# A hybrid encoder trunk on one core: products b^T a of the WKV chunks made in the preparation and kept in DRAM, and both prompt jobs' inverses, first merges and loads placed among the last v products

## The chip, the cores and the metric

The kernel runs on one core of one Trainium2 chip. A core has TensorE (PE: matmuls; PEld: its weight loads), VectorE (DVE), ScalarE (ACT), GpSimd (POOL) and SyncE (SP), which here only issues DMA transfers; ACT and POOL issue some too. Each engine works through its own queue in order. The metric is the device time of one execution in microseconds (us), as the median of several runs. The kernel before takes 4056.93 us (three runs, 4045.68 to 4063.49).

## The reference

Two batches, a prompt of 256 tokens and a sample of 1024 tokens, pass through two layers with the same weights: RWKV-7 time mixing and an MLP, then neighbourhood attention and an MLP, all in float32. The change touches the time mixing alone. It ends in a scan over the tokens, run forwards and backwards for each of 16 heads of 64 channels:

```python
def step(S, inp):
    r_t, w_t, k_t, v_t, a_t, b_t = inp
    sa = jnp.einsum('bhvk,bhk->bhv', S, a_t)
    S = S * w_t[:, :, None, :] + sa[..., None] * b_t[:, :, None, :] + v_t[..., None] * k_t[:, :, None, :]
    return S, jnp.einsum('bhvk,bhk->bhv', S, r_t)
...
for d in range(2):
    w_lora = jnp.tanh(xw @ w1[d]) @ w2[d]
    decay = jnp.exp(-jnp.exp(-jax.nn.softplus(-(w0[d] + w_lora).astype(f32)) - 0.5))
    iclr = _heads(jax.nn.sigmoid((a0[d] + (xa @ a1[d]) @ a2[d]).astype(f32)))
    k_d = kf * (1.0 + (iclr - 1.0) * k_a_h)
    y = y + _wkv_scan(rf, _heads(decay), k_d, vf, -kk, kk * iclr, reverse=(d == 1))
```

## The kernel before

The projections come first; then a **preparation** makes, for 8 pairs of heads m and 2 directions d, four tensors of 128 channels by tokens (b, k, a and r, each scaled by cumulative decays) and stores them in the DRAM tensor `x_d`. It works in 48 units h (pair h // 6, token segment of 256, 512 or 512 tokens, direction h % 2). Between the units stand the r products (`rps`, three matmuls for each float32 product, L108 to L110) and, from unit 42.5 on, the 40 blocks of v products (`vps`, 24 matmuls each, L530 to L532), which go on when the units are done. All this is placed by a list `self.cq` of (time in units, function): it is sorted, and what it calls is the written order of PE, DVE, ACT and POOL (`manual_schedule`). SP is not in that set; its order comes from the scheduler.

The **scan** cuts tokens into chunks of 64. Within a chunk the recurrence is solved as a triangular system: its matrix is built from the 64 x 64 products b^T a of the chunk, and its inverse Q is needed before the chunk's step. Ten jobs of 16 chunks follow each other: jobs 0 and 1 hold the prompt (4 pairs with 4 chunks each), jobs 2 to 9 the sample of one pair each. Each job has 16 steps, and each step handles one chunk forwards and one backwards for both heads of the pair (or of a prompt pair). What a job needs is placed in a second list, `todo`, by time in steps (job j at 16 j, earlier parts at negative times):

- `load` (L844): a and b of 4 chunks from `x_d` into `eab`, 256 KB, four buffers; eight loads per job.
- `early` (L850): b^T a, eight matmuls of 64 x 64 into the PSUM tile `aps` per load (each float32 matmul shows as two rows); `keep` (L854) copies them to `za` on ACT; `store` (L857) writes them to the DRAM tensor `dd` of the job.
- `mload` (L877): the 32 x 32 diagonal blocks of a job's systems are gathered from `dd`, one system on each partition, into `mt` and `mraw`; `mtr` (L882) transposes `mraw` into `mt` on POOL in four pieces.
- `rank1` (L895 to L901): the inverse of all 32 x 32 blocks in 31 steps on DVE, 60 instructions.
- `qst` (L909 to L912): the inverses go to the DRAM tensor `qd`, transposed by POOL as well; `qld` (L927, L928) loads them into `Q` and `qx` in 12 transfers of 64 KB in pieces of 32 numbers.
- `merge1`, `merge2` (L940 to L954): the 64 x 64 inverse from its 32 x 32 blocks, with `za` and `qx`, eight groups per job on PE and ACT (`yps`, `qps`).
- `kload`, `decay` (L966, L971): k, b, a, r of 4 chunks into `x` (512 KB), and the decay matrix into its fifth part by POOL; `uvload` and `vload` (L979, L1017): v from DRAM.
- `kprod`, `kcopy`, `kmask` (L995, L1005, L1000): products of each pair of chunks into the one PSUM tile `kps`, copied by ACT (`ll`) and masked by DVE (`zz`).

The step itself is a chain on PE and ACT: `bx` and `by` matmuls (L1033), the copies `up` (L1074, one per step), `uv` (L1086) and `S` (L1099). The output is normed and stored by `scan_post`, and gate, output projection, MLP and layer 1 follow.

When `begin` runs (unit 52, after v block 15), the preparation's memory is released, the scan's first tiles are opened in `er` (the pool that exists while v products still run; the pool `rp` opens after them), and what job 0 needs up to its inverse is moved from `todo` into `cq`, spread over the last v blocks.

Of the kernel before, what the change touches and what calls it, by code (L numbers as in the profile page):

```python
# [5 lines left out]
F32 = mybir.dt.float32  # L6
# [7 lines left out]
P = 128  # L14
# [4 lines left out]
L = 64  # L19
# [42 lines left out]
class Trunk:  # L62
# [50 lines left out]
    def l0_proj(self):  # L113
# [267 lines left out]
        for h in range(N):  # L381
# [99 lines left out]
        def begin():  # L481
            bctx.close()
            self.scan_begin()

            hi, c = -6.0, ((-46.0, tb), (-22.0, tb + 6.0), (-6.0, tb + 17.0))
            for x in self.todo:
                if x[3] < 3 and x[0] <= hi:
                    (x0, t0), (x1, t1) = c[:2] if x[0] < -22.0 else c[1:]
                    t = t0 + (t1 - t0) * (x[0] - x0) / (x1 - x0)
                    self.cq.append((max(t, t1 - 3.0 + 0.01 * x[0]) if x[3] == 2 else t, x[1], x[2]))  # L490
            self.todo = [x for x in self.todo if x[3] == 3 or x[0] > hi]
            self.cq.sort(key=lambda x: x[:2])
# [169 lines left out]
    def prep_products(self, U, h, i):  # L662
# [52 lines left out]

    def prep_bonus(self, U, h, step):
# [20 lines left out]
    def scan_begin(self):  # L737
# [8 lines left out]
        self.r_v, self.r_q, self.r_x = ([[er.tile(shape, F32, name=name + "0")], 0] for name, shape in  # L746
                                        (("vv", [P, 16, 64]), ("qq", [P, 16, 2, 64]), ("qx", [P, 16, 2, 32])))
        self.r_e = [[er.tile([P, 2, 4, 64], F32, name=f"eab{i}") for i in range(4)], 0]
        self.r_za = [[er.tile([P, 4, 64], F32, name=f"za{i}") for i in range(9)], 0]
# [5 lines left out]
        self.todo = []  # L755
# [7 lines left out]
    def scan_until(self, t, level=3):  # L763
        todo = [x for x in self.todo if x[0] <= t and x[3] <= level]
        self.todo = [x for x in self.todo if x[0] > t or x[3] > level]
        for x in todo:
            x[2]()

    def scan(self):
# [3 lines left out]
        def grow(r, name, shape, n=1):  # L773
# [1245 lines left out]
```

## Time and profile before

| what | us |
|---|---|
| median of three runs | 4056.93 |
| profiled execution, its own time | 4067.45 |
| profiled execution, span from first to last instruction | 4065.7 |
| preparation up to the first v block | about 317 to 559 |
| v blocks | 559.4 to 715.1 |
| first step of the scan (first copy `up`) | 764.3 |
| last step of the scan | 1360.0 |

Over the whole span PE is busy for 92%, DVE 62%, ACT 37%, POOL 35%. A busy time is the union of an engine's instructions; matmuls overlap, so a busy PE is not PE at its peak. The rows that follow below are of four kinds: stretches with the busy time of each engine, the granted TensorE clock (1.00 is 2.4 GHz, 0.50 is 1.2 GHz) and the share of the DMA engines; single instructions in order of time; the chain of waits, which says what released what; and DMA transfers by line, with the time from issue to landing.

### The profile page before, as it was taken

What the parts mean: (1) busy time and instruction counts of PE and PEld (TensorE: products, weight loads), DVE (VectorE), ACT (ScalarE), POOL (GpSimd) and SP (SyncE); (2) the same over time, 40 slices, a digit from 0 to 9 for tenths busy, and PEclk for the clock granted to TensorE, in tenths of its full rate; (3) what the DMA queues carried; (4) which work ended last, traced back from release to release, by engine and by line L of the source; (5) the groups of instructions that cost most, each with busy time, mean ns of one, the idle gap of its engine ahead of it and who ended that gap; (6) DMA issues with size and microseconds to landing.
All of it is one profiled execution on the core that took longest, in us unless ns stands there. A gap on an engine that the chain in (4) does not pass through costs nothing.

```text
span 4065.7 us, 82648 instructions
## 1 busy us (share of the span) xinstructions
PE 3743.1 (92%) x33028; PEld 3107.9 (76%) x33028; DVE 2508.8 (62%) x4771; ACT 1512.1 (37%) x3587; POOL 1412.1 (35%) x1402
## 2 busy tenths in 40 slices
PE   7888979688788799999999989999989999999999
PEld 4665659566667688888888879777768788888888
DVE  7898973477686447555555561466674755555555
ACT  6776652344444441121111132456564211111111
POOL 4450000245455534222222250455553422222222
PEclk8997889799999899999999999999989999999999
DMA  3326655888876431111111115343343111111101
GB/s 109 88 81 220 210 188 159 196 212 198 197 197 155 139 120 32 37 42 42 32 42 42 37 62 175 84 90 82 71 117 130 48 41 42 37 37 42 42 32 63
DMA packets 405745, 403.44 MB, mean 99 GB/s; under 512 B 163152, under 2 KB 328240, under 8 KB 404080
## 3 DMA queue, kind: packets, MB, share of 16 engines
q1 hardware_dynamic: 349488, 318.31, 28.6%
q10 hardware_dynamic: 46704, 61.35, 4.4%
q0 software_dynamic: 9168, 18.49, 1.7%
q8 instruction: 259, 4.24, 0.5%
q14 instruction: 126, 1.03, 0.1%
HBM read 288.03 MB, written 121.24 MB: 101 GB/s over the span
## 4 chain that ended last, share of the span: by engine, by line
PE 69%; DVE 14%; ACT 6%; issue 4%; DMA 4%; POOL 3%; SPq 0%; ACTq 0%; DVEq 0%; POOLq 0%
PE ps L108 18%; PE ps L109 17%; PE ps L110 17%; PE kps L995 3%; PE bx L1033 2%; PE by L1033 2%; PE vps L530 1%; PE vps L531 1%; PE vps L532 1%; PE op L1933 1%; DVE mu L199 1%; DVE q L901 1%; DVE tmp L899 1%; PE pt L1875 1%; ACT ll L1005 1%
## 5 line engine op out<-in xcount | busy, mean ns | idle before, releaser
L1480 DVE TENSOR_TENSOR x<-ps,x 128x256 f32<-128x256 f32 x1488 | 813.1, 595 | 609.9 <-PE ps L110 609.5
L103 POOL TENSOR_TENSOR wlo<-raw,whi 128x1024 fp32r<-128x1024 f32 (+1 forms) x178 | 390.7, 2195 | 851.2 <-ACT whi L102 824.4
L108 PE MATMUL ps<-ahs,whi 128*128 128x512 f32 x1536 | 612.8, 399 | 0.0
L109 PE MATMUL ps<-als,whi 128*128 128x512 f32 x1536 | 599.3, 390 | 0.0
L110 PE MATMUL ps<-ahs,wlo 128*128 128x512 f32 x1536 | 598.9, 390 | 0.0
L108 PE MATMUL ps<-hh,whi 128*128 128x512 f32 (+1 forms) x1536 | 545.2, 355 | 12.2 <-DVE x L1480 12.1
L109 PE MATMUL ps<-hl,whi 128*128 128x512 f32 (+1 forms) x1536 | 544.0, 354 | 0.0
L110 PE MATMUL ps<-hh,wlo 128*128 128x512 f32 (+1 forms) x1536 | 543.9, 354 | 0.0
L102 ACT CAST whi<-raw 128x1024 fp32r<-128x1024 f32 (+1 forms) x206 | 201.3, 977 | 692.4 <-PE ps L109 634.4
L1459 POOL TENSOR_TENSOR rl<-rl 128x512 f32<-128x512 f32 (+1 forms) x192 | 174.5, 909 | 489.9 <-PE ps L110 450.7
L108 PEld LDWEIGHTS ps<-ahs,whi 128*128 128x128 f32 x1536 | 288.7, 188 | 62.3 <-issue 6.9
L110 PEld LDWEIGHTS ps<-ahs,wlo 128*128 128x128 f32 x1536 | 288.5, 188 | 61.8
L108 PEld LDWEIGHTS ps<-hh,whi 128*128 128x128 f32 x1536 | 290.4, 189 | 55.9 <-DVE x L1480 15.6
L109 PEld LDWEIGHTS ps<-als,whi 128*128 128x128 f32 x1536 | 288.8, 188 | 53.2 <-issue 1.0
L110 PEld LDWEIGHTS ps<-hh,wlo 128*128 128x128 f32 x1536 | 290.3, 189 | 40.6
L109 PEld LDWEIGHTS ps<-hl,whi 128*128 128x128 f32 x1536 | 290.3, 189 | 40.3
L1458 ACT ACTIVATE rl<-ps 128x512 f32<-128x512 f32 (+1 forms) x192 | 100.8, 525 | 532.8 <-PE ps L110 532.8
L995 PE MATMUL kps<-x 64*64 64x192 f32 (+1 forms) x2560 | 204.9, 330 | 27.9 <-DVE zz L1000 16.2
L1461 ACT CAST hh<-rl 128x512 fp32r<-128x512 f32 (+1 forms) x192 | 105.5, 550 | 321.7 <-POOL rl L1459 321.7
L108 PE MATMUL ps<-ahp,whi 128*128 128x256 f32 x768 | 222.4, 290 | 0.8 <-DVE ot L1363 0.8
L110 PE MATMUL ps<-ahp,wlo 128*128 128x256 f32 x768 | 215.6, 281 | 1.5 <-POOL wlo L103 1.5
L109 PE MATMUL ps<-alp,whi 128*128 128x256 f32 x768 | 215.3, 280 | 0.0
(334 smaller groups left out, 8384.5 us busy)
## 6 DMA issues: line engine op xcount, KB each, us to landing
x<-x_d SPq DMA_DIRECT2D x88, 512.0 KB, 6.8
raw<-in_w_down_dram SPq DMA_DIRECT2D x64, 512.0 KB, 3.6
raw<-in_w_up_dram SPq DMA_DIRECT2D x64, 512.0 KB, 3.4
eab<-x_d SPq DMA_DIRECT2D x80, 256.0 KB, 5.1
x_d<-ar ACTq DMA_DIRECT2D x32, 512.0 KB, 3.0
x_d<-bk ACTq DMA_DIRECT2D x32, 512.0 KB, 3.9
bs<-tab SPq DMA_DIRECT2D x128, 96.0 KB, 4.9
v_d<-vt ACTq DMA_DIRECT2D x80, 128.0 KB, 3.9
```

Source lines behind the costliest of these rows:

```text
L102: nc.scalar.copy(hi[:, cs], raw)
L103: lo_eng.tensor_tensor(out=lo[:, cs], in0=raw, in1=hi[:, cs].bitcast(F32), op=ALU.subtract)
L108: mm(ps, sh, mh, start=first, stop=False)
L109: mm(ps, sh, ml, start=False, stop=False)
L110: mm(ps, sl, mh, start=False, stop=last)
L199: nc.vector.scalar_tensor_tensor(out=v, in0=sm, scalar=hm[:, i[j] * 8 + k:i[j] * 8 + k + 1], in1=v, op0=ALU.mult, op1=ALU.add)
L995: mm(J["kp"][out, e, 192 * c + 192 - w:192 * c + 192], x[es, b, 2 * pr + c], x[es, 5 - w // 64:5, 2 * pr + c], start=True, stop=True)
L1033: mm = lambda out, a, b, start, stop: nc.tensor.matmul(out, a, b, start=start, stop=stop, skip_group_check=True)
L1458: nc.scalar.activation(r[:, :n], ps[:, :n], AF.Relu)
L1459: nc.gpsimd.tensor_tensor(out=r[:, :n], in0=r[:, :n], in1=r[:, :n], op=ALU.mult)
L1461: nc.scalar.copy(hh[:, :n], r[:, :n])
L1480: nc.vector.tensor_tensor(out=xv, in0=ps[:, :n], in1=xv, op=ALU.add)
```

## The change

- **Products in the preparation.** A new DRAM tensor `za_d` holds b^T a for all pairs, directions and tokens. `prep_system` makes them in each unit: matmuls into a PSUM tile of the ring that the preparation's other matmuls use (tag `l2`, four buffers), one or two ACT copies of 256 columns, one or two DMA stores of 128 KB issued by POOL. `load`, `early`, `keep`, `store`, the tiles `eab` and the tensors `dd` are gone.
- **Reading them.** `zload` brings `za` of 4 chunks from `za_d` (128 KB, eight per job, six buffers). `mload` gathers the diagonal blocks from `za_d` in pieces of 32 numbers: eight transfers for a sample job, 32 for a prompt job, where it was four. `mt` and `mraw` are half as wide.
- **The start of the scan.** For jobs 0 and 1 `mload`, `mtr`, `rank1` and `qst` are put on the list `ahead`, which `begin` adds to `cq` at fixed times in units; so are job 0's `qclear`, `qld`, `vload`, and the merges and loads of its first two groups. The step of the list for the inverses is 4.5 units.
- **Buffers.** `er` has two tiles of `x`, one of `uv`, one of `yt` per direction, which join the rings; the last job uses none of them. The second `kd` buffer of direction 1 goes. The first merges have a PSUM pool of their own (`pmB`).

```diff
@@ in the preparation's list
             at(h + 1.191, self.prep_store, U, h, nc.scalar)
+            for i, t in enumerate((1.3, 1.75, 1.76)):
+                at(h + t, self.prep_system, U, h, i)
@@ begin
             bctx.close()
+            self.pm = vctx.enter_context(tc.tile_pool(name="pmB", bufs=2, space=PSUM))
             self.scan_begin()
-            hi, c = -6.0, ((-46.0, tb), (-22.0, tb + 6.0), (-6.0, tb + 17.0))
...
+            self.cq += [(tb + t, 1000 + i, f) for t, i, f in self.ahead]
             self.cq.sort(key=lambda x: x[:2])
@@ prep_open, prep_products
+        self.za_d = self.dram("za_d", [8, 2, P, T])
...
-            u["kd"] = pk.tile([P, 512], F32, name="kd", tag=f"kd{d}", bufs=2)
+            u["kd"] = pk.tile([P, 512], F32, name="kd", tag=f"kd{d}", bufs=2 - d)
@@ new
+    def prep_system(self, U, h, step):
+
+        nc, u = self.nc, U[h]
+        m, d, c0, c1, w = self.prep_unit(h)
+        if step == 0:
+            u["ps"] = self.ppl.tile([P, 512], F32, name="sps", tag="l2")
+            for c in range(w // L):
+                t = slice(c * L, c * L + L)
+                for es, eo in HALVES:
+                    nc.tensor.matmul(u["ps"][eo, t], u["bk"][es, 0, t], u["ar"][es, 0, t], start=True, stop=True)
+            return
+        for c in range(0, w, 256):
+            if step == 1:
+                u["za", c] = self.pk.tile([P, 256], F32, name="pza", tag="pza", bufs=2)
+                nc.scalar.copy(u["za", c], u["ps"][:, c:c + 256])
+            else:
+                nc.gpsimd.dma_start(self.za_d[m, d, :, c0 + c:c0 + c + 256], u["za", c])
@@ scan_begin, scan
-        self.r_e = [[er.tile([P, 2, 4, 64], F32, name=f"eab{i}") for i in range(4)], 0]
-        self.r_za = [[er.tile([P, 4, 64], F32, name=f"za{i}") for i in range(9)], 0]
+        self.r_za, self.r_x4, self.r_uv = ring("za", [P, 4, 64], 2), ring("x4", [P, 5, 4, 64], 2), ring("uv", [P, 8, 2, 64], 1)
+        self.r_yt = [ring(f"yt{d}", [P, 4, 64], 1) for d in range(2)]
...
-        grow(self.r_za, "za", [P, 4, 64], 12)
+        grow(self.r_za, "za", [P, 4, 64], 4)
@@ scan_job
+        pre = lambda t, f: self.ahead.append((t, len(self.ahead), f))
...
-            def early(c, x, d=d, g=g):
-                es, eo = HALVES[x]
-                if c == x == 0:
-                    J["pa"] = w4(self.pa.tile([P, 512], F32, name="aps", tag="aps"))
-                mm(J["pa"][eo, c], J["e", d, g][es, 0, c], J["e", d, g][es, 1, c], start=True, stop=True)
...
-                    nc.sync.dma_start((mt, raw)[d][o:o + 32, 32 - 32 * b:2080 - 32 * b], J["dd"][d][:, :, 32 * b:32 * b + 32].rearrange("c e s t -> (c e) (s t)"))
+                    for e in range(2):
+                        o = 64 * d + 32 * b + 16 * e
+                        for m, c0, k, n in parts:
+                            src = self.za_d[m, d, 64 * e + 32 * b:64 * e + 32 * b + 32].rearrange("s (c t) -> c s t", t=L)
+                            nc.sync.dma_start((mt, raw)[d][o + k:o + k + n], src[c0:c0 + n, :, 32 * b:32 * b + 32])
...
+        if j < 2:
+            T1, T2, T3, step, put = *((0.2, 3.0, 7.6), (8.0, 10.8, 15.4))[j], 4.5, pre
+        else:
+            T1, T2, T3, step, put = -25.2, -21.73, -9.7, 12.0, at
+        put(T1, mload)
...
+            def zload(d=d, g=g, m=m, c0=c0):
+                J["za", d, g] = self.nxt(self.r_za, left)
+                nc.sync.dma_start(J["za", d, g], self.za_d[m, d, :, tok(c0)].rearrange("p (c t) -> p c t", c=4))
...
+            t, put = 2 * n - 5, at
+            if j == 0 and n < 2:
+                t, put = 12.5 + n, pre
...
+            put(8.5 + 0.1 * n if put is pre else 2 * n - 9.5, zload)
...
+            put(10.1 + 0.1 * n if put is pre else 4 * (n // 2) - 8.5 + n % 2, kload)
+            put(10.3 + 0.1 * n if put is pre else 2 * n - 6.4, decay)
+            put(8.7 + 0.1 * n if put is pre else 4 * (n // 2) - 4.3 + 0.1 * (n % 2), uvload)
```

Three places in the written order follow. The first is PE's queue in the preparation, where two units' input products (`l<-tw`, `l<-ta`), the key norms (`kb`) and the r products (`rps`) alternate. Before:

```order
L110 MATMUL rps<-mh_233,wl 128x512
L633 MATMUL l_4619<-tw,wa 128x512
L633 MATMUL l_4622<-tw,wa 128x512
L633 MATMUL l_4626<-ta,wa 128x512
L633 MATMUL l_4630<-ta,wa 128x512
L707 MATMUL kb<-kr,heads 128x512
L108 MATMUL rps<-mh_189,wh 128x256
```

The same place now:

```order
L110 MATMUL rps<-mh_233,wl 128x512
L631 MATMUL l_5061<-tw,wa 128x512
L631 MATMUL l_5064<-tw,wa 128x512
L631 MATMUL l_5068<-ta,wa 128x512
L631 MATMUL l_5072<-ta,wa 128x512
L723 MATMUL sps<-ar,bk 64x64 x16
L705 MATMUL kb<-kr,heads 128x512
L723 MATMUL sps<-ar,bk 64x64 x8
L108 MATMUL rps<-mh_189,wh 128x256
```

Two units' b^T a (`sps`, 8 matmuls for 256 tokens and 16 for 512) now stand around `kb` and ahead of the next r products; they read `ar` and `bk`, which DVE writes.

The second place is SP's queue from the middle of the v blocks to the first loads of `x`: `wraw` are v weights, `qd` the stored inverses. Before:

```order
L877 DMA mt<-dd 32x2048
L877 DMA mraw<-dd 32x2048 x2
L410 DMA wraw<-in_w_v_dram 128x512
L844 DMA eab_6424<-x_d 128x2x256
L410 DMA wraw<-in_w_v_dram 128x512
L909 DMA qd<-q 128x1024
L912 DMA qd<-qt 128x1024
L928 DMA qq_6419<-qd 32x16x32 x2
L927 DMA qx_6420<-qd 32x16x32 x3
L928 DMA qq_6419<-qd 32x16x32
L857 DMA dd<-za_6433 128x4x64
```

Now:

```order
L901 DMA qd<-q 128x1024
L904 DMA qd<-qt 128x1024
L866 DMA mraw<-za_d 4x32x32 x8
L866 DMA mt<-za_d 4x32x32 x16
L936 DMA za_7353<-za_d 128x256
L936 DMA za_7354<-za_d 128x256
L984 DMA uv_7357<-v_d 64x4x128 x2
L1022 DMA vv_7350<-v_d 64x4x64 x8
L922 DMA qx_7352<-qd 32x16x32
L923 DMA qq_7351<-qd 32x16x32
...
L923 DMA qq_7351<-qd 32x16x32 x5
L971 DMA x_7355<-x_d 128x4x256
```

The loads of job 0's inverses (`qx`, `qq`) followed the stores of `qd` at once; now 24 of job 1's 32 gathers and 12 loads of `za`, `uv` and `vv` stand between them, and the first load of `x` stands behind all of these. The 32 gathers of job 0 are further up, where the loads of `eab` and `vv` were, ahead of the loads `wraw` that were issued at 636.56 us.

The third place is POOL's queue around the two inverses. Before:

```order
L882 COPY mt<-mraw 64x8x32 x4
L910 COPY qt<-q 128x8x32 x4
L870 MEMSET q 128x1024
L871 MEMSET q 128x32
...
L971 TENSOR_TENSOR x_7407<-cst,dall 64x256 x2
L882 COPY mt<-mraw 64x8x32 x4
L971 TENSOR_TENSOR x_7408<-cst,dall 64x256 x2
L971 TENSOR_TENSOR x_7409<-cst,dall 64x256 x2
```

Now:

```order
L870 COPY mt<-mraw 64x8x32 x4
L902 COPY qt<-q 128x8x32 x4
L856 MEMSET q 128x1024
L857 MEMSET q 128x32
L870 COPY mt<-mraw 64x8x32 x3
L976 TENSOR_TENSOR x_7355<-cst,dall 64x256 x2
L870 COPY mt<-mraw 64x8x32
L976 TENSOR_TENSOR x_7356<-cst,dall 64x256 x2
L902 COPY qt<-q 128x8x32 x4
```

The last quarter of job 1's transposing (`mt<-mraw`) now stands behind the decay matrix of `x_7355`, the first group's tile, which waits for that tile's load. On DVE all 60 instructions of job 1's inverse now stand ahead of the first mask `zz`; before, 13 of them stood ahead of it and the rest between the masks.

## Rows read from the trace of the kernel before

**Rows 1.** stretches: us, busy of PE, PEld, DVE, ACT, POOL; clock, DMA share, GB/s

```profile
360.00:540.00 180.00, 164.75 (x1049) 113.36 (x1048) 176.88 (x319) 125.55 (x268) 0.00 (x0) 0.88 0.60 206
540.00:610.00 70.00, 45.69 (x272) 36.86 (x271) 48.05 (x85) 36.20 (x75) 0.00 (x0) 0.78 0.61 190
610.00:715.00 105.00, 102.71 (x960) 100.53 (x960) 35.81 (x85) 21.80 (x54) 11.50 (x16) 0.98 0.55 157
715.00:764.00 49.00, 21.72 (x394) 19.66 (x392) 15.81 (x32) 8.71 (x24) 13.07 (x29) 0.55 0.83 201
822.00:1194.00 372.00, 306.78 (x8909) 254.62 (x8904) 282.35 (x624) 174.01 (x666) 194.36 (x284) 0.95 0.83 202
1194.00:1310.00 116.00, 99.69 (x2780) 83.14 (x2780) 86.23 (x188) 54.87 (x211) 62.12 (x88) 0.97 0.68 158
```

**Rows 2.** copies `up` that begin jobs 0, 1, 7, 9: start, us, instruction

```profile
764.28 0.27 ACT L1074 COPY up<-bx 128x128 f32<-128x128 f32 x1
821.96 0.27 ACT L1074 COPY up<-bx 128x128 f32<-128x128 f32 x1
1193.80 0.27 ACT L1074 COPY up<-bx 128x128 f32<-128x128 f32 x1
1310.28 0.27 ACT L1074 COPY up<-bx 128x128 f32<-128x128 f32 x1
```

**Rows 3.** chain of waits by line, jobs 1 to 6, then 7 and 8

```profile
by line: PE kps L995 18.8%; PE bx L1033 13.3%; PE by L1033 12.2%; issue 9.7%; DVE q L901 5.1%; DVE tmp L899 4.8%; ACT ll L1005 4.5%; DVE zz L1000 3.7%; ACT up L1074 3.0%; DMA qq<-qd 2.8%; DVE mu L1164 2.2%; PE zps L1200 1.8%; PE aps L850 1.
by line: PE kps L995 20.6%; PE bx L1033 14.5%; PE by L1033 13.8%; issue 9.1%; DVE q L901 6.2%; DVE tmp L899 5.7%; ACT ll L1005 5.3%; ACT up L1074 4.7%; DVE zz L1000 3.3%; PE zps L1200 2.6%; ACT y L1107 1.8%; ACT y L1104 1.5%; DVE mu L1164 1
```

**Rows 4.** PE in order of time, two series of b^T a

```profile
645.82 0.68 PE L850 MATMUL aps<-eab 64*64 64x64 f32 x16
722.72 3.40 PE L850 MATMUL aps<-eab 64*64 64x64 f32 x48 [5.18 <-DMA eab<-x_d]
```

**Rows 5.** stretch, instructions on `aps` alone: PE, PEld, ACT

```profile
822.00:1194.00 372.00, 35.97 (x771) 30.53 (x768) 17.49 (x48) 0.95 0.83 202
```

**Rows 6.** DVE in order of time: weights, both inverses, first mask

```profile
649.25 1.41 DVE L420 TENSOR_TENSOR wl<-wraw,wh 128x512 fp32r<-128x512 f32 x2 [9.84 <-ACT wh L415]
680.80 0.29 DVE L895 SCALAR_TENSOR_TENSOR q<-mt,q 128x31 f32<-128x31 f32 x1 [7.24 <-POOL mt L882]
705.13 0.25 DVE L895 SCALAR_TENSOR_TENSOR q<-q,mt 128x31 f32<-128x31 f32 x1
746.32 0.72 DVE L895 SCALAR_TENSOR_TENSOR q<-mt,q 128x31 f32<-128x31 f32 x1 [40.94 <-POOL mt L882]
754.32 0.68 DVE L1000 TENSOR_TENSOR zz<-kps,cst 128x512 f32<-128x512 f32 x1
```

**Rows 7.** SP's issues in order of time

```profile
626.46 9.10 SPq L1017 DMA_DIRECT2D vv<-v_d  x8
636.56 3.23 SPq L410 DMA_DIRECT2D wraw<-in_w_v_dram  x2
707.72 0.32 SPq L912 DMA_DIRECT2D qd<-qt  x1
```

**Rows 8.** POOL in order of time

```profile
678.66 2.11 POOL L882 COPY mt<-mraw 64x256 f32<-64x256 f32 x4 [53.48 <-DMA mraw<-dd]
719.29 1.29 POOL L971 TENSOR_TENSOR x<-cst,dall 64x256 f32<-64x256 f32 x2
```

**Rows 9.** DMA issues, jobs 1 to 6: KB each, median us to landing

```profile
x<-x_d SPq DMA_DIRECT2D x48, 512.0 KB, 7.4
eab<-x_d SPq DMA_DIRECT2D x48, 256.0 KB, 5.7
qq<-qd SPq DMA_DIRECT2D x48, 64.0 KB, 4.2
```

**Rows 10.** SP's issues by line: ns min/median/max of one, first and last start

```profile
L1827 SPq DMA_DIRECT2D bpm<-tab x112: 302/422/1813, 2604.3 to 2975.5; - x112
...
L928 SPq DMA_DIRECT2D qq<-qd x80: 315/494/3538, 708.1 to 1289.1; - x80
```

More of the change, by code (lines that the diff above doesn't have):

```diff
@@ L482, in begin @@
             bctx.close()
+            self.pm = vctx.enter_context(tc.tile_pool(name="pmB", bufs=2, space=PSUM))
             self.scan_begin()
-            hi, c = -6.0, ((-46.0, tb), (-22.0, tb + 6.0), (-6.0, tb + 17.0))
[L486 to L491, printed above, removed]
+            self.cq += [(tb + t, 1000 + i, f) for t, i, f in self.ahead]
             self.cq.sort(key=lambda x: x[:2])
@@ L754, in scan_begin @@
         self.jobs[0:0] = [[(4 * h + g, 0) for g in range(4)] for h in range(2)]
-        self.todo = []
+        self.todo, self.ahead = [], []
         for j in range(10):
@@ L761, in scan_begin, with yt_fill @@
         self.todo.sort(key=lambda x: x[:2])
[L763 to L767, printed above, removed]
+    def yt_fill(self, i):
+        for d in range(2):
+            hi = slice(32 - 32 * d, 64 - 32 * d)
+            for t in self.r_yt[d][0][i:]:
+                self.nc.gpsimd.memset(t, 0.0)
+                for e in range(2):
+                    rows = slice(64 * e + hi.start, 64 * e + hi.stop)
+                    self.nc.gpsimd.tensor_copy(t[rows, :, hi], self.ident[rows, rows].unsqueeze(1).to_broadcast([32, 4, 32]))
     def scan(self):
@@ L807, in scan, with at, nxt @@
         with tc.manual_schedule(engines=order):
-            self.scan_until(1e9)
+            for x in self.todo:
+                x[2]()
         self.sctx.close()
-    def at(self, t, f, level=3):
-        self.todo.append((t, len(self.todo), f, level))
-    def nxt(self, r):
+    def at(self, t, f):
+        self.todo.append((t, len(self.todo), f))
+    def nxt(self, r, left=False):
+        if left and r[2]:
+            er, i = r[0][:r[2]], r[1] % len(r[0])
+            r[:] = [t for t in r[0][i:] + r[0][:i] if not any(t is x for x in er)], 0, 0
         t = r[0][r[1] % len(r[0])]
@@ L822, in scan_job @@
         B = 16 * j
-        at = lambda t, f, level=3: self.at(B + t, f, level)
+        at = lambda t, f: self.at(B + t, f)
+        pre = lambda t, f: self.ahead.append((t, len(self.ahead), f))
+        left = j == len(self.jobs) - 1
         mm = nc.tensor.matmul
@@ L830, in scan_job @@
         c4 = lambda t: t.rearrange("p (c t) -> p c t", c=4)
[L833 to L865 removed]
         def mload():
[L868 removed]
+            mt, raw = (self.er.tile([P, 32, 32], F32, name=nm, tag=nm) for nm in ("mt", "mraw"))
             q = self.er.tile([P, 32, 32], F32, name="q", tag="q")
@@ L901, in rank1 @@
                 nc.vector.tensor_tensor(out=q[:, 0:jj, jj:], in0=q[:, 0:jj, jj:], in1=tv, op=ALU.add)
-            at(T2 + pace * int(12 * sum(cost[jj + 1:]) / sum(cost)), rank1, E)
+            x = sum(cost[jj + 1:]) / sum(cost)
+            put(T2 + (int(12 * x) if j > 1 else step * x), rank1)
         def qst(i):
@@ L913, in scan_job @@
         for i in range(4):
-            at(T3 + 0.1 * i, lambda i=i: qst(i), E)
+            put(T3 + 0.1 * i, lambda i=i: qst(i))
         def qclear():
@@ L949, in merge2 @@
                 if c == x == 0:
-                    J["qps", d, g] = w4(self.pa.tile([P, 512], F32, name="qps", tag="aps"))
+                    J["qps", d, g] = w4((self.pm if j == 0 and n < 2 else self.pa).tile([P, 512], F32, name="qps", tag="aps"))
                 mm(J["qps", d, g][es, c, :32], J["yt", d, g][es, c], J["Q"][es, 4 * g + c, d, hi], start=True, stop=True)
@@ L975, in uvload @@
                 if d == 0:
-                    J["uv", g] = self.nxt(self.r_uv)
+                    J["uv", g] = self.nxt(self.r_uv, left)
                 p = g if d == 0 else 3 - g
@@ L1017, in vload @@
                 nc.sync.dma_start(J["v"][eo, k:k + n], vd[rows, m * P + 64 * e:m * P + 64 * e + 64].rearrange("(c s) v -> s c v", s=L))
-        at(-6.1, lambda: vload(0))
-        at(-5.423, lambda: vload(1))
+        for e, t in enumerate((-6.1, -5.423)):
+            if j == 0:
+                pre(8.9 + 0.1 * e, lambda e=e: vload(e))
+            else:
+                at(t, lambda e=e: vload(e))
         def yalloc():
```

94 lines of the change are left out of this document (32 added, 62 removed).

## The prediction

> **What bounds the kernel now.** I read the stretches first, then single instructions around the change, then the chain of waits. The change touches three stages, each with another limit.
>
> In the preparation (360 to 540 us) DVE is busy for 176.88 of 180 us: it is the bound. PE is close behind with 164.75, but at a granted clock of 0.88 of 2.4 GHz; ACT has 125.55, POOL nothing [rows 1]. The reader is to see that two engines are nearly full there, and that the change adds work to the second.
>
> Between the last v product (715) and the first step (764.28) PE is busy for 21.72 of 49 us, at 0.55 of its clock [rows 1, 2]. This stretch is a chain of waits: the second inverse starts only at 746.32, after 40.94 us in which DVE waited for the transposed systems; the first had run from 680.80 to 705.13 beside the v products [rows 6]. The first mask follows at 754.32, and the first step 10 us later.
>
> In the scan jobs 1 to 6 take (1193.80 - 821.96) / 6 = 62.0 us each, jobs 7 and 8 (1310.28 - 1193.80) / 2 = 58.2 [rows 2]. The products b^T a run three jobs ahead (their time is -43 steps), so in jobs 7 and 8 nearly none are left. PE is busy for 82 and 86% there, and DMA for 83 and 68% [rows 1]. In the chain of jobs 1 to 6 stand 1.6% or more of `aps` and 2.8% of `qq<-qd`, the loads of the inverses; neither is among the first lines of jobs 7 and 8 [rows 3].
>
> **Part by part: the scan.** Removed from every job are eight loads of 256 KB, 128 PE rows of `aps`, eight ACT copies and eight stores; added are eight loads of 128 KB and four more gathers. For six jobs `aps` costs PE 35.97 us and ACT 17.49 [rows 5]. What of it lies on the path? The chain gives 372 us x (1.6% + 2.8%) = 16 us [rows 3]; the jobs that go without give 6 x (62.0 - 58.2) = 22 us [rows 2]; all of PE's rows would be 36 us. The lower bound is the `aps` share alone, 6 us, if the loads of the inverses stay late. I take 22: it is a measurement of the same step without these parts, though job 8 also lacks the inverse in its last ten steps. Jobs 0 and 7 I leave at nothing: job 0 trades the end of job 1's inverse for cold loads, below. The larger rings for `x` (8 for 6) and `uv` (3 for 2) go into this term unpriced.
>
> The gathers now read pieces of 128 bytes where they read 8 KB. `qq<-qd` has such pieces, 64 KB to a transfer, and lands in 4.2 us [rows 9]. Eight issues of 0.49 us [rows 10] and one landing are 8 us; between the gather (-25.2) and the first step of the inverse (-21.73) lie 3.5 steps of 3.7 us, 13 us. So I cost it at nothing, and 5 us for each of eight jobs if SP comes late. The Trainium skill (DMA: Bandwidth & Descriptors, Specifications) states that a transfer needs 512 bytes or more for line rate; that speaks against these gathers. By the row a 64 KB transfer in 128-byte pieces indeed takes 4.2 us, against 5.7 for 256 KB of `eab` [rows 9], so per byte the trace agrees; the room of 13 us is why the sum stays the same.
>
> **The start of the scan.** I follow the new order. Job 0's 32 gathers stand where `vv` and `eab` stood. An issue of a 16 KB transfer takes 0.42 us (median), one of `qq` 0.49 [rows 10], one of the eight `vv` 9.10 / 8 = 1.14 [rows 7]. A gather is nearest to the first: 32 x 0.42 = 13.5 us from about 623 (four issues ahead of the `vv` at 626.46), so the next weights go out at 636.5, where they go out now (636.56) [rows 7]. The first inverse stands behind their splits on DVE, which end at 649.25 + 1.41 = 650.7 [rows 6]; it starts there, 30 us earlier than now, since the chain through `eab`, `aps`, `za` and `dd`, for which POOL waited 53.48 us [rows 8], is gone. It takes 705.38 - 680.80 = 24.6 and ends at 675.3. From its end to the second store of `qd` are 708.04 - 705.38 = 2.7 us [rows 7]: 678.0. Then SP issues 24 gathers of job 1 (10.1), twelve loads of `za`, `uv`, `vv` (12 x 0.49 = 5.9) and twelve of the inverses (5.9): 699.9. Now the load of the first `x`, 7.4 us to landing [rows 9]: 707.3. POOL makes its decay matrix (1.29) and only then the last quarter of the transposing (2.11 / 4) [rows 8]: 709.1. So job 1's inverse starts at 709 rather than at 746, takes 24.6, and ends at 733.7. The first mask stands behind it, and from mask to first step I keep 10 us: 743.7. The v products end near 715 as before (eight series `aps` leave, four series `sps` and the first merges come, about 3 us each way), so PE waits 20 us for the masks. The gain is 764.3 - 743.7 = 20 us. Every issue at 0.32 [rows 7] would make it 27; every one at 1.14 would put the first step at some 800, 35 later than now.
>
> The second `x` tiles, `za` and `lnx` now stand on SP behind the stores of job 1's inverse, which wait for DVE: they go out near 737 and land at 745, when the second step wants them. I add 3 us for job 0's first steps (0 to 10).
>
> **The preparation.** 80 series of 16 rows are added to PE, 55 of them in the 33 units between 360 and 540. One series takes 0.68 us at the full clock and 3.40 / 3 = 1.13 at the half [rows 4]. PE's 164.75 us at 0.88 are 145 at the full clock; with 55 x 0.68 = 37 it has 182 for the 180 that DVE needs: just too much. At the present mean clock it would be 164.75 + 37 / 0.88 = 207, 27 us over. Each series waits for DVE's `ar` and `bk`, and behind it on PE are `kb` and the r products, for which ACT and DVE wait in their turn; that couples the two full engines, with about a unit (5.5 us) of slack. The bounds are 0 and 27, and 90 us (80 x 1.13) if nothing were hidden and the clock low. I take 8: nearer to 0, since the pauses in which PE now waits are filled first. A rule would make it 0: the Trainium skill (TensorE: Matmul & The Clock Gate, What's actually happening) says that the throttled state is the default and activity releases it. The 49 us in which PE was busy for 21.72 us show 0.55, and the v products, with 102.71 of 105, show 0.98 [rows 1]; by that the added rows would pay for themselves with a higher clock, and the time would be 4018, inside the forecast's range.
>
> ACT's copies of 256 columns take 17.49 / 48 = 0.36 us [rows 5]; 55 are 20 us on top of 125.55 of 180 [rows 1]: hidden beside DVE. The stores go through POOL, which is idle there. From 540 to 610 DVE and PE are busy for 48 and 46 of 70 us [rows 1], so the last units' products cost nothing. The single `kd` buffer of direction 1 I cost at nothing: ACT writes it 0.8 unit after DVE is through with it; without that slack it is 0.6 us for each of 24 units.
>
> **Sum**, against the profiled execution's 4067.45 us: -20 (start) + 3 (job 0) - 22 (scan) + 8 (preparation) = -31, so 4036. That execution lies 0.26% above the median 4056.93; scaled by it, 4026. Everything after the scan stands in the same order.
>
> **Rivals.**
> *The preparation becomes PE's* (13%). For it: 182 of 180 us at the full clock, and the clock is not full. Against it: low clock and waits go together. 27 instead of 8: -12, 4045.
> *The start does not come earlier* (8%). SP has some 80 issues ahead of the first `x`, and the two inverses run one after the other. `vv` at 1.14 us speaks for it, the medians against it. The term -20 falls away: -11, 4046.
> *More comes back in the scan* (21%). With DMA at 68% instead of 83% and larger rings, loads are no longer late: the chain's unexplained waiting ("issue", 9.7%, 36 us [rows 3]) halves, and the preparation costs nothing: -20 + 3 - 22 - 18 = -57, 4000. Against it: jobs 7 and 8 have 9.1% as well.
> *Slower* (8%). The series in the preparation stall PE in order, it stands idle before each, and the clock stays at 1.2 GHz: up to 80 x 1.13 = 90 us, all exposed since DVE waits for `kb`: -20 + 3 - 22 + 90 = +51, 4107. It decides from 59 us of the 90 on, where the kernel would be 20 us slower than now. Against it: r products fill the time between.
>
> **How the numbers follow.** The forecast (50%) has the range 4008 to 4044. A measurement of this kernel tells 0.5%, 20 us, from no change: faster is below 4037, slower above 4077. A fifth of the forecast (10%) lies above 4037; with the first two rivals that is 31% for the same, 40% + 21% = 61% for faster, 8% for slower. The range 3994 to 4060 leaves out the slower case and the better part of the fourth.
>
> **What would show it.** Right: the first `up` near 744 to 752 with the second inverse ending just before the first mask; jobs 1 to 6 at about 58 us; the v products starting less than 10 us later than 559. Wrong: DVE in the preparation below 90% busy and waiting for PE (the second rival's sign is SP issuing for over 50 us between the inverses); jobs 1 to 6 still at 61, with `qq<-qd` on the chain, would mean that the loads of the inverses were late for another reason than `aps`.

## The result: slower by 0.4%

The changed kernel took 4068.58 us (median of 15 runs), the kernel before 4056.36 beside it: a ratio of 1.0037, interval 1.0023 to 1.0052 (a ratio here is not the quotient of the two medians, which is 1.0030). In a second comparison it was 4069.58 against 4054.09, 1.0048 (1.0030 to 1.0066). One of its ten executions took 12854.6 us at a mean granted clock of 0.27; the ratio leaves it out, and without it the median is 4067.28. Forecast were 4026 us and a gain; the loss is 12 to 15 us by the medians, 15 to 19 by the ratios. By the prediction's own limits (faster below 4037, slower above 4077) this is no change, to which it gave 31%, but 4068.58 lies above both of its ranges, 4008 to 4044 and 3994 to 4060.

The profile after, stretch by stretch. First the stretches that answer to [rows 1] (preparation, v products, jobs 1 to 6):

```profile
360.00:540.00 180.00, 166.57 (x1666) 121.53 (x1666) 154.22 (x273) 118.11 (x277) 25.81 (x48) 0.91 0.64 218
596.10:772.00 175.90, 143.24 (x1307) 138.56 (x1306) 89.92 (x201) 48.53 (x112) 23.71 (x44) 0.87 0.48 142
840.60:1208.70 368.10, 310.56 (x8136) 259.68 (x8135) 279.33 (x625) 160.70 (x617) 195.74 (x287) 0.93 0.74 162
```

DVE, which was the bound of the preparation with 176.88 us, has 154.22, and PE is not full either: nobody is the bound. That is the prediction's own sign that the preparation's term is wrong. The copies `up` of jobs 0, 1, 7 and 9, as in [rows 2]:

```profile
783.16 0.27 ACT L1082 COPY up<-bx 128x128 f32<-128x128 f32 x1
840.58 0.27 ACT L1082 COPY up<-bx 128x128 f32<-128x128 f32 x1
1208.65 0.27 ACT L1082 COPY up<-bx 128x128 f32<-128x128 f32 x1
1329.40 0.27 ACT L1082 COPY up<-bx 128x128 f32<-128x128 f32 x1
```

The first step comes 19 us later than before, and jobs 1 to 6 take 61.3 us each, not 58. The instructions of the first key product (`kb`) and the first v product, each with the start of its first and last row:

```profile
L705 PE MATMUL kb<-kr,heads x48: 374/587/1215, 319.3 to 620.3; 16*128 16x512 f32 x32, 16*128 16x256 f32 x16
L527 PE MATMUL vps<-wh,mh x320: 278/283/582, 596.1 to 771.6; 128*128 128x256 f32 x160
```

From these and the `up` copies I cut every trace into three stretches: preparation (first `kb` to first v product, 596.1 - 319.3 = 276.8), start (first v product to first `up`), scan (first to last `up`). The columns to the right are the median of the executions and the ratio to the kernel before, which ran beside each (medians 4054.09 to 4056.67). e2, e4, e5 and e8 have four executions each, the others six or more, where the table does not say otherwise.

| run | preparation | start | scan | median us | ratio (interval) |
|---|---|---|---|---|---|
| before | 238.2 | 204.9 | 595.8 | 4056.36 | 1 |
| before again (e14, e15) | 238.7, 237.3 | 201.4, 202.4 | 590.8, 587.7 | 4053.37, 4056.31 | one execution each |
| changed | 276.8 | 187.0 | 596.7 | 4068.58 | 1.0037 (1.0023 to 1.0052) |
| changed again (e11) | 274.5 | 186.7 | 572.7 | 4069.58 | 1.0048 (1.0030 to 1.0066) |
| e1 no products | 239.4 | 187.0 | 586.4 | 4054.36 | 0.9999 (0.9986 to 1.0011) |
| e2 products alone | 275.3 | 185.8 | 598.5 | 4080.68 | 1.0074 (1.0057 to 1.0091) |
| e3 products of constants | 250.6 | 185.4 | 588.5 | 4047.98 | 0.9988 (0.9974 to 1.0002) |
| e4 no hold | 277.3 | 187.5 | 578.8 | 4076.35 | 1.0065 (1.0050 to 1.0080) |
| e5 products later | 278.0 | 187.8 | 588.4 | 4081.40 | 1.0060 (1.0038 to 1.0082) |
| e6, e12 no gathers | 276.4, 273.7 | 189.7, 189.1 | 569.3, 571.5 | 4063.62, 4060.45 | 1.0022 (1.0006 to 1.0039), 1.0017 (1.0004 to 1.0030) |
| e7 before, no aps | 237.0 | 203.6 | 578.4 | 4045.75 | 0.9970 (0.9957 to 0.9984) |
| e8 inverse loads first | 276.1 | 198.8 | 581.3 | 4082.23 | 1.0062 (1.0046 to 1.0077) |
| e9 stores on SP | 260.0 | 186.1 | 580.1 | 4052.63 | 1.0004 (0.9993 to 1.0015) |
| e10 e9 and e5 | 253.0 | 185.6 | 580.8 | 4044.54 | 0.9982 (0.9970 to 0.9995) |
| e13 before, stores on SP | 236.5 | 202.6 | 594.4 | 4049.69 | 0.9986 (0.9972 to 1.0000) |

The reader is to see which columns can be trusted. The preparation repeats within 3 us from one execution to the next, the start within 4; the same scan varies by 24 us, so it needs means or medians. With the means of the complete kernels (for the scan before 592.2, from the first trace, e13, e14 and e15; for the changed one 583.7, from the first trace, e5, e9, e10 and e11) the change is +38 (preparation), -16 (start), -8 (scan): +14, near the loss that the medians show. The -8 is known to some 5 us only, and what follows the scan takes 2700 to 2708 us from one of these traces to the next; that the sum comes so close is luck in part.

### The profile page after: what moved, and what is told of

Read it like the earlier page. It is cut to its first block, busy times and chain, and to the rows that moved or that the text cites. A ratio compares the mean times of both kernels' runs of the same rounds, so it can differ in the third digit from the quotient of the medians.

```text
span 4080.3 us, 82931 instructions
## 1 busy us (share of the span) xinstructions
PE 3782.0 (93%) x33028; PEld 3149.8 (77%) x33028; DVE 2503.6 (61%) x4771; ACT 1509.0 (37%) x3587; POOL 1456.0 (36%) x1488
## 4 chain that ended last, share of the span: by engine, by line
PE 70%; DVE 11%; ACT 6%; issue 5%; DMA 4%; POOL 3%; SPq 1%; ACTq 0%; DVEq 0%; POOLq 0%
PE ps L108 17%; PE ps L109 17%; PE ps L110 17%; PE kps L1000 3%; PE by L1041 2%; PE bx L1041 2%; PE vps L527 1%; PE vps L528 1%; PE vps L529 1%; PE op L1941 1%; DVE mu L199 1%; PE pt L1883 1%; DVE ll L287 1%; ACT ll L1010 1%; PE sps L723 1%
## 5 line engine op out<-in xcount | busy, mean ns | idle before, releaser
L1000 PE MATMUL kps<-x 64*64 64x128 f32 (+1 forms) x2560 | 211.6, 337 | 30.2 <-DVE zz L1005 13.7
L1005 DVE TENSOR_TENSOR zz<-kps,cst 128x512 f32<-128x512 f32 x160 | 110.3, 689 | 177.9 <-ACT ll L1010 176.9
```

Of the source, the lines that this page charges most:

```text
L1000: mm(J["kp"][out, e, 192 * c + 192 - w:192 * c + 192], x[es, b, 2 * pr + c], x[es, 5 - w // 64:5, 2 * pr + c], start=True, stop=True)
L1005: nc.vector.tensor_tensor(out=z, in0=src[:, :, :, :P], in1=self.mask[d].unsqueeze(1).unsqueeze(1).to_broadcast([P, 2, 2, P]), op=ALU.mult)
```

## The experiments

**The preparation: what do the products cost, and by what?** e1 to e4 keep the 80 stores but take them from a tile of zeros (with it the preparation itself starts 7 to 12 us later, so their stretches are compared rather than their times).

```diff
-  nc.gpsimd.dma_start(self.za_d[m, d, :, c0 + c:c0 + c + 256], u["za", c])
+  nc.gpsimd.dma_start(self.za_d[m, d, :, c0 + c:c0 + c + 256], self.pre["zero"])
```

e4 has no other edit but a single tile `pza`. e2 also leaves out the copies, e1 the copies and the products. e3 is e2 with this one:

```diff
-  nc.tensor.matmul(u["ps"][eo, t], u["bk"][es, 0, t], u["ar"][es, 0, t], start=True, stop=True)
+  nc.tensor.matmul(u["ps"][eo, t], self.ident[es, 0:64], self.ident[es, 0:64], start=True, stop=True)
```

> The changed kernel without the products in the preparation: no sps rows on PE, no copies on ACT; the 80 stores go out as before, from a tile of zeros that nobody waits for (so the scan reads zeros in the products' place). Everything else stands where the change put it. Theory A (the 1280 rows cost their whole length, because PE in the preparation cannot put them into its pauses): the first v product starts near 560 us instead of 596.1, the first up copy at 747 instead of 783.2, and the time is 36 us below the changed kernel's, about 4032. Theory B (the copies and rows cost little, the lengthening is the stores' traffic or the single kd buffer, which stay): the v products start at 585 or later and the time is within 12 us of the changed kernel's.

> As e1, but the 1280 rows stand on PE with their operands, in the same place and the same four PSUM buffers; nobody copies them out, and the stores take the tile of zeros. Theory A1 (PE's length decides: 50 us of rows at the clock of the stretch): v products start near 590 to 596, as in the changed kernel. Theory A2 (the wait of the copies for the stores, 33 us on ACT, decides, since the PSUM buffers are held until then): near 565, and the rows alone cost under 10 us.

> As e2, but each row multiplies two slices of a constant, so that the rows wait for nothing that DVE makes; place and number are the same. If the wait of the rows for bk (25 us in the profile) costs what it shows, the v products start 15 to 25 us earlier than in e2; if PE's length alone decides, within 5 us of e2.

> As e2 with the copies out of PSUM back on ACT, into one tile that no store reads; the stores take the tile of zeros. Theory A1: as e2 plus what ACT's copies cost, v products at 590 to 596, the time as the changed kernel's. Theory A2 (stores hold the two buffers): 33 us of ACT's waiting are gone, v products at 565 to 572, the time 25 to 30 us below the changed kernel's.

e1: 239.4, as before: the stores' traffic and the single `kd` buffer cost nothing, theory B falls. (Its time came down by 14 us only, of 25 that the stretch and the later start leave; what follows its scan was the longest of all traces, 2711 us, and the rest is not explained.) e2: 275.3, all of the loss, without a copy and without a store that holds anything; e4 adds 2, within what one execution differs from the next. So my first theory of the trace, that ACT's waits for the stores of `pza` decide, fell: in the changed kernel they show 18.5 us (between 400 and 530), and without them e4 takes as long, 277.3. Where ACT does not wait for these stores it waits for PE instead; in e2, same stretch:

```profile
ACT lw L634 <- PE l L633: 50.0, 11, 7.4
```

e3: the same rows on the same PSUM buffers, but 250.6. PE's length costs 12 us; the other 25 are there only when the rows read `ar` and `bk`.

**Who waits for whom.** In e3 PE has nearly no room left (125.56 of 130 us), and its clock is 0.97:

```profile
400.00:530.00 130.00, 125.56 (x1352) 90.97 (x1351) 124.78 (x225) 88.50 (x190) 0.00 (x0) 0.97 0.59 205
```

In the changed kernel, the products in the same stretch (busy us, mean ns, idle time of PE ahead of them), to be laid beside [rows 4]:

```profile
L723 PE MATMUL sps<-ar,bk 64*64 64x64 f32 x528 | 22.4, 239 | 10.2 <-DVE bk L688 6.9 <-ACT pr L441 2.8
```

The waits there (sum in us, times, longest):

```profile
ACT pza L728 <- DMA za_d<-pza: 18.5, 10, 3.4
ACT lw L632 <- PE l L631: 17.9, 6, 5.3
DVE bk L682 <- DMA x_d<-bk: 8.2, 6, 2.4
PE sps L723 <- DVE bk L688: 6.9, 5, 2.2
DVE pkk L708 <- PE kb L705: 5.6, 3, 3.5
```

PE waits for DVE, ACT for PE, DVE for a store and for PE. Before, the wait of DVE for its store was this:

```profile
DVE bk L684 <- DMA x_d<-bk: 0.4, 1, 0.4
```

One turn of it in the changed kernel, in order of time:

```profile
409.84 1.97 PE L723 MATMUL sps<-ar,bk 64*64 64x64 f32 x32 [2.80 <-ACT pr L441]
414.74 0.68 DVE L688 SCALAR_TENSOR_TENSOR bk<-tha,emc 128x512 f32<-128x512 f32 x1
420.25 0.70 PE L631 MATMUL l<-tw,wa 64*128 64x256 f32 x4
420.98 0.84 ACT L632 ACTIVATE lw<-l,hw 128x256 f32<-128x256 f32 x2 [5.27 <-PE l L631]
421.91 0.48 ACTq L712 DMA_DIRECT2D x_d<-bk  x1
427.68 0.69 DVE L682 TENSOR_TENSOR bk<-kd,emc 128x512 f32<-128x512 f32 x1 [2.35 <-DMA x_d<-bk]
436.33 0.85 PE L723 MATMUL sps<-ar,bk 64*64 64x64 f32 x16 [0.99 <-DVE bk L688]
```

`bk` is complete at 415.42, but its store is issued at 421.91: it stands in ACT's queue behind the tanh of a later unit, which waits 5.27 us for PE's `l` rows, and these come later because PE has stood before the products. The store lands late, and DVE, which has two `bk` buffers, must wait for it before it writes the next; then PE waits for DVE again. In other turns ACT waits for the store of `pza` in this place, which e2 and e4 show not to matter. From the end of `bk` to the issue of its store pass 0.8 us before, 2.7 in the changed kernel, 2.6 in e2, 0.8 in e3 (means over units 8 to 39). That is a circle of three engines, and two links can be cut without leaving work out.

e5 moves the products behind the r products:

```diff
-            for i, t in enumerate((1.3, 1.75, 1.76)):
+            for i, t in enumerate((1.6, 2.05, 2.06)):
```

> The changed kernel, complete, with the products of a unit 0.3 step later in the preparation's order (1.6 for 1.3, copies and stores 0.3 later too). On PE they then stand behind the r products of the pair, which wait for nothing, instead of ahead of them. Theory A (PE waits in order for bk: 25 of the 37 us): from the first key product to the first v product 250 us as in e3, instead of 277, and the time about 25 us below the changed kernel's, 4043. Theory B (length, or the four PSUM buffers that are shared): at least 270 us, and the time within 8 us of the changed kernel's, 4061 or more.

278.0: a miss for theory A as I had it. PE no longer stood before the products, but the wait went on round the circle; in e5, same stretch:

```profile
ACT lw L632 <- PE l L631: 18.5, 5, 6.0
DVE bk L682 <- DMA x_d<-bk: 15.3, 8, 4.0
```

DVE's wait for the store nearly doubled, and the issue came 4.2 us after `bk`. (The median of e5, of four executions, lies 12 us above the changed kernel's, against what either theory expected; its trace has no stretch that shows it, and that stays open. The same holds for e8, which has this edit too.) e9 cuts the other link:

```diff
-            at(h + 1.191, self.prep_store, U, h, nc.scalar)
+            at(h + 0.575, self.prep_store, U, h, nc.sync)
```

> The changed kernel, complete, with the stores of ar and bk in the preparation issued by SP right behind bk (0.575 step) instead of by ACT at 1.191, where they stand behind ACT's tanh of later units. Theory E (the 25 us beyond PE's length are a circle: PE waits for bk, ACT for PE's l rows, the store behind ACT, DVE for the store before it may write bk again): DVE's wait for the store (8.2 us between 400 and 530 in the changed kernel) falls below 3, first key product to first v product 255 to 265 us instead of 277. Theory F (the circle has only PE and DVE, the store is late because all is late): 272 or more, the time within 6 us of the changed kernel's.

> e9 and e5 together: the stores on SP and the products behind the r products. Theory E: both links are out, only PE's length is left, 250 us as in e3, and the time about 25 us below the changed kernel's, 4044. Theory F: 272 or more, 4065 or more.

e9: the store is issued 0.1 us after `bk`, DVE's wait for it is gone from the list of waits, the preparation takes 260.0 and the time falls by 16 us. e10, with both links cut: 253.0, 4044.54, 25 us below the changed kernel as expected, and 0.18% below the kernel before. Its stretch:

```profile
400.00:530.00 130.00, 128.58 (x1320) 88.93 (x1318) 122.89 (x219) 93.97 (x222) 20.41 (x38) 1.00 0.71 241
```

and its products, before which PE does not stand idle:

```profile
L723 PE MATMUL sps<-ar,bk 64*64 64x64 f32 x624 | 23.1, 222 | 0.0
```

PE is busy for 128.58 of 130 us at the full clock: only now is it the bound that the first rival spoke of. So e5's edit is worth nothing alone and 7 us once the store is out of the way. e13 makes e9's edit in the kernel before, to see whether it helps without the circle:

> The kernel before, complete, with e9's edit alone: the stores of ar and bk issued by SP right behind bk. Theory E (the late store is a link of the changed kernel's circle; before, DVE waited 0.4 us for it between 400 and 530): within 4 us of the kernel before, 238 us from the first key product to the first v product. Rival (ACT is freed of two issues a unit, which helps by itself, and e9 shows only that): 8 us or more below the kernel before.

The preparation is 1 to 2 us shorter, the time 5 us (0.9986, an interval that ends at 1): of the 16 us that the edit gives the changed kernel, about 11 are then the circle's. That is a difference of medians, and 5 us lie between what theory E (within 4) and its rival (8 or more) expected; the preparation says it more clearly, 15 to 17 us shorter by this edit in the changed kernel, 1 to 2 before. Between e10 and e13 the intervals overlap: that the products in the preparation gain anything over the store's edit alone is not shown.

**The scan.**

e6 and e12 put this ahead of the gathers in `mload` of the changed kernel:

```diff
+            if j > 1:
+                nc.sync.dma_start(raw[64:128].rearrange("p s t -> p (s t)"), self.a["w_r"][j - 2, 64:128, 0:1024])
+                nc.sync.dma_start(mt[0:64].rearrange("p s t -> p (s t)"), self.a["w_r"][j - 2, 0:64, 0:1024])
+                return
```

e7 changes `early` and `keep` of the kernel before:

```diff
+                if j > 1:
+                    return
...
-                nc.scalar.copy(J["za", d, g], J["pa"])
+                (nc.scalar.copy(J["za", d, g], J["pa"]) if j < 2 else nc.scalar.activation(J["za", d, g], J["e", d, g][:, 0], AF.Copy, scale=0.0))
```

e11 is the changed kernel, e14 and e15 the kernel before, without an edit.

> The changed kernel with the eight gathers of each sample job's system replaced by two loads of rows of 4 KB from a weight matrix (so these jobs invert other numbers); the prompt jobs and the preparation are as in the changed kernel. Theory C (the gain in the scan was eaten by SP's queue: issues of qx and qq behind the gathers, 15.7 us of the chain of jobs 1 to 6): jobs 1 to 6 at about 58.5 us, the time about 20 us below the changed kernel's, 4048. Theory D (what was counted as the price of aps is DVE's and POOL's work on the norm and the inverse, which stays): jobs 1 to 6 at 60 to 62 us, the time within 8 us of the changed kernel's.

> The kernel before with the 128 rows of aps left out in each of the eight sample jobs (ACT makes za from the loaded tile, times zero, in the same place; loads, stores and gathers stay). The prediction's step (aps and what it delays cost 22 us in jobs 1 to 6): the time about 20 us below the kernel before, 4035, jobs 1 to 6 at 58 to 59 us. Theory D (PE has room for them in the pauses in which it waits for DVE): within 8 us of the kernel before.

> The changed kernel once more, beside e12, to see how far two executions of the same scan lie apart: the preparation within 3 us of 277, the scan from the first to the last up copy anywhere from 579 to 599 us, since the runs so far with the same scan lie there.

> e6 once more (two loads of 4 KB rows for the eight gathers of each sample job), with more rounds, on the same chip as e11. Theory C (SP's queue behind the gathers eats the gain): at least 12 us below e11 in the medians, and the scan at 565 to 575 us. Theory D: less than 6 us below e11.

> The kernel before once more, for the spread of its scan from one execution to the next. If the changed scan is faster by what e7 and e12 leave (about 5 us), this one lies with 595.8 of the first trace in a band of some 26 us whose middle is near 590, as the changed kernel's nine lie between 573 and 599 about 586; the prediction's 22 us would need 600 to 615.

> As e14, a third trace of the same scan: 577 to 603 us about a middle near 590 by e7 and e12, 600 to 615 by the prediction.

e7: without `aps` the kernel before is 11 us faster, half of the predicted 22; between what the step and theory D expected. e6 and e12: without the gathers the changed kernel is 5 and 9 us faster by the medians (the latter side by side, 4060.45 against 4069.58; 7 against the 4067.28), with intervals that touch or overlap, again between theories C and D. The scan of e12, 571.5, is what theory C expected, but that of e11, with the gathers, is 572.7, so these two traces tell nothing. Out goes `aps` with 11, in come the gathers with 5 to 9: that leaves 2 to 6, and the traces' means say 8. e14 and e15 put the scan before at 588 to 596, not at the 600 to 615 that 22 us would need. Neither theory is right alone; the split between what the gathers cost and the work of DVE and POOL is known to some 5 us, not better. The chain of waits of jobs 1 to 6 in the changed kernel, to be laid beside [rows 3]:

```profile
by line: PE kps L1000 17.1%; PE by L1041 11.8%; PE bx L1041 11.2%; issue 10.0%; DVE tmp L890 4.7%; DVE q L892 4.7%; ACT ll L1010 3.5%; DVE zz L1005 3.1%; ACT up L1082 2.7%; DVE mu L1172 2.3%; SPq L922 2.3%; DMA x<-x_d 2.1%; POOL x L976 2.0%
```

`aps` and `qq<-qd` have left the first places; issues of SP (`qx`, L922) and loads and decay matrices of `x` stand there instead. But this is the longest scan of the complete changed kernels. In e11, the shortest, neither the issues nor the loads are among the first places:

```profile
by line: PE kps L1000 19.3%; PE bx L1041 12.7%; PE by L1041 12.0%; issue 9.3%; DVE q L892 5.6%; DVE tmp L890 5.3%; ACT ll L1010 5.0%; ACT up L1082 4.1%; DVE zz L1005 3.6%; DVE mu L1172 2.4%; PE zps L1208 2.3%; POOL x L976 2.1%; POOL y L1203
```

`tmp` and `q`, the inverse on DVE, are about as large as before in both. How the gathers cost their time is not separated: e6 and e12 take away their issues and their traffic together, and the scheduler gave SP another order with it. In the changed kernel the next job's last four gathers, a load of `x` and two of `uv` stand between the stores of an inverse and its first load; in e12 a single load does. And SP reaches these stores early in the changed kernel and stands there in order, with the loads behind them, until DVE is through; in jobs 1 to 6 of the changed kernel, then of e12:

```profile
SPq L901 <- DVE q L886: 86.8, 6, 16.7
SPq L905 <- DVE q L890: 9.6, 6, 1.9
```

**The start.**

e8 is e5 with these two:

```diff
-                pre(T3 + 1.5 + 0.1 * i, lambda x=(d, b, e): qld(*x))
+                pre(T3 + 0.31 + 0.01 * i, lambda x=(d, b, e): qld(*x))
-            T1, T2, T3, step, put = *((0.2, 3.0, 7.6), (8.0, 10.8, 15.4))[j], 4.5, pre
+            T1, T2, T3, step, put = *((0.2, 3.0, 7.6), (8.65, 10.8, 15.4))[j], 4.5, pre
```

> As e5, and at the start of the scan job 0's loads of its inverse and of za stand ahead of job 1's 32 gathers instead of behind them. Then PE need not wait some 16 us among the last v products for qx. If the first step hangs on the second inverse, as the prediction had it, the first up copy comes as long after the first v product as in e5 or a few us later (187 us in the changed kernel), and the time is that of e5 within 5 us; if it hangs on the v products, it comes 10 to 16 us earlier and so does the end.

In the changed kernel SP, PE and DVE stand like this, in order of time:

```profile
655.05 27.22 SPq L866 DMA_DIRECT2D mraw<-za_d  x16
682.38 6.37 SPq L866 DMA_DIRECT2D mt<-za_d  x16
694.19 0.27 DVE L886 SCALAR_TENSOR_TENSOR q<-mt,q 128x31 f32<-128x31 f32 x1
717.91 0.25 DVE L886 SCALAR_TENSOR_TENSOR q<-q,mt 128x31 f32<-128x31 f32 x1
747.18 0.27 DVE L886 SCALAR_TENSOR_TENSOR q<-mt,q 128x31 f32<-128x31 f32 x1 [23.51 <-DMA za<-za_d]
756.20 1.06 PE L942 MATMUL yps<-qx,za 64*64 64x32 f32 x16 [15.19 <-DMA qx<-qd]
769.92 0.25 DVE L886 SCALAR_TENSOR_TENSOR q<-q,mt 128x31 f32<-128x31 f32 x1
```

PE stands for 15.19 us among the v products, since the loads of `qx` are behind 24 gathers and 12 other loads. In e8 that wait is gone and the v products take 160.6 us instead of 175.8, but the second inverse starts at 771.73, 23 us later than in e5, counted from the first v product:

```profile
771.73 0.72 DVE L886 SCALAR_TENSOR_TENSOR q<-mt,q 128x31 f32<-128x31 f32 x1 [44.41 <-POOL mt L870]
795.47 0.27 ACT L1082 COPY up<-bx 128x128 f32<-128x128 f32 x1
```

The first `up` comes 198.8 us after the first v product, 11 later than in e5. So to take PE's 15 us away brings nothing as long as the second inverse comes later for it; how late the gathers push it I had expected too small ("a few us"). What the first step hangs on without this edit, the end of the chain of waits in e11 shows:

```profile
768.96 2.10 POOL qt L902 x4
771.07 0.34 SPq L904
773.98 3.58 DMA za<-za_d
780.83 0.27 ACT up L1082
```

The transposed second inverse (`qt`) is stored by SP, the loads of `za` stand behind that store, and when they have landed the merges, products of `kps` and the first `up` follow. e1 and e5 have the same chain. In the trace of the changed kernel above, in e9 and in e10 it comes to these loads from the end of the v products instead; there the store is issued at 772.46 and the v products end at 772.1. So the second inverse and the v products, with PE's wait in them, are through at nearly the same time; that one of them alone would not move the first step by much follows from this, but no run tested it.

## Why the prediction was wrong, point by point

- **The preparation, +8; measured +38. This is the step that failed.** Its count of PE's work was good: "182 for the 180" and 8 us stand against 12 in e3. What failed is the sentence "I take 8: nearer to 0, since the pauses in which PE now waits are filled first". The products wait themselves, in PE's order; the prediction saw that ("that couples the two full engines, with about a unit (5.5 us) of slack") but priced the coupling at nothing and left one member out, the store in ACT's queue. It costs 25 us, 22 to 24 of which e10 takes back by cutting two links. The first rival had the place and, with 27, the nearest size, but not the cause: PE is not full in the changed kernel. The slower case had the cause ("stall PE in order"), at more than twice the size, and with a clock that did not fall (0.91 for 0.88). With the other terms as forecast, 38 would have made the time about that of the kernel before (-20 + 3 - 22 + 38 = -1); it became slower because the scan gave less than was set against it.
- **The clock.** The Trainium skill (TensorE: Matmul & The Clock Gate, What's actually happening) was quoted for a preparation that pays for its rows with a higher clock. The trace agrees where PE is kept busy: 1.00 in e10, where an r product's row takes 359 ns; in the changed kernel, where PE stands, the clock is 0.91 and the row takes 387. But the rows did not pay for themselves even there: at 1.00 in e10, and at 0.97 in e3, the preparation is 15 and 12 us longer than before, so the time of 4018 that was worked out from the rule would not have come without the circle either.
- **ACT's copies, POOL's stores and the `kd` buffer at nothing: right.** e4 against e2 gives 2 us, e1 against before 1.
- **The scan, -22; measured about -8** (-7 in jobs 1 to 6, 61.4 to 60.2 each, -2 in job 0, where +3 was forecast). The lower bound of the text, 6, was nearer. Jobs 7 and 8 were a poor measure. They are indeed shorter than jobs 1 to 6, by 2.5 to 3.8 us each in the four traces before, so the 22 were no accident of one trace; but in the five of the changed kernel, where no job has `aps`, they are still shorter, by 1.0 to 2.7. So a good part of the difference was never the price of `aps`: e7 without its matmuls gains 11. That job 8 lacks the inverse is a likely reason, which no run tested. And the gathers, costed at nothing because they are early enough for the inverse, cost 5 to 9, with the order of SP's loads that came with them.
- **The start, -20; measured -16: right in size, in part by luck.** Counted from the first v product, the first inverse was expected from 91 to 116 us and ran from 98 to 122, the second from 150 to 174 and ran from 151 to 174, the first `up` was expected at 184 and came at 187. The way there was another one. The first 32 gathers took 33.7 us on SP, not 13.5, which made the first inverse 7 us late; job 1's 24 took 24.2, not 10.1. SP's waits in the gathers, from 650 to 690 and from 720 to 780:

```profile
SPq L866 <- DMA v_d<-vt: 18.0, 7, 8.4
SPq L866 <- DMA v_d<-vt: 14.8, 7, 5.2
```

These are stores of v issued by ACT, which the gathers neither read nor write over. In the records of the trace the gathers at 673.25, 675.80, 678.47 and 681.22 each wait for, and then raise, the completion semaphore that such a store, issued 2.0 to 2.6 us before, had raised. So over half of this time is not the price of an issue, which the sum took from other rows, but waiting for another engine's store. The second inverse was on time all the same, because what the prediction put between the gathers and it, 21 us of loads, a decay matrix and the last quarter of the transposing, was not in the way:

```profile
734.59 10.45 SPq L866 DMA_DIRECT2D mt<-za_d  x16
736.28 1.29 POOL L976 TENSOR_TENSOR x<-cst,dall 64x256 f32<-64x256 f32 x2
737.52 0.66 POOL L870 COPY mt<-mraw 64x256 f32<-64x256 f32 x1
760.97 1.20 SPq L971 DMA_DIRECT2D x<-x_d  x2
```

The decay matrix and the last quarter were done before the first load of `x` was issued, and the inverse started at 747.18, 2 us after the last gather went out. That this decay matrix waits for that tile's load, as the text on the written order and the prediction have it, is wrong. Nor did the v products end as before: they took 20 us longer, 15 of them PE's wait for `qx`.

## What to carry to other kernels

Where an engine is given work that waits for another full engine, do not ask only whether its busy time still fits: follow the circle of who then waits for it, DMA issues in the queues of computing engines included, and price one turn. A store that frees a buffer stood badly here behind work that waits for other engines: to move it to SP gave 16 us in the changed kernel, and 5 in the one before, hardly more than none. And before a gain is read from one stretch of a trace, see by how much that stretch differs in a second execution.

## What was not expected of the hardware

The same instructions of the scan took 572.7 and 596.7 us in two executions of one kernel, while the preparation repeated within 3 us and the start within 4. Among the last v products gathers on SP waited 18.0 us for stores of ACT whose data they do not touch; where I followed it, both used the same completion semaphore. And with PE at 128.58 of 130 us, the granted clock was 1.00 over the whole stretch, against 0.91 with 119.63.
